# A mixture-of-experts stage with its chunk order changed: large and small experts in turn, down blocks queued behind

## The chip, the cores and the metric

The kernel runs on one core of a Trainium2 chip. The metric is the device time of one execution in microseconds (us). The engines are TensorE (PE, with its weight loads as PEld), VectorE (DVE), ScalarE (ACT), GpSimd (POOL) and SyncE (SP), whose queue (SPq) issues the loads from HBM.

## The reference

The program is a two-layer decoder trunk over 256 positions of width 1024. What matters here is the expert stage of the second layer and the gated embedding behind it:

```
logits = xt @ w_router;  gates = softmax(top-2 logits)
for each of 8 experts e, on the positions routed to it:
    g, u = split(xb @ w_gate_up[e])        # 1024 -> 2 x 3584
    y    = (silu(g) * u) @ w_down[e]       # 3584 -> 1024
h = h + sum of gate * y
h = h + (p @ w_proj) * sigmoid(rmsnorm(h) @ w_gate)
out = rmsnorm(h)
```

All of it is float32.

## The kernel before

**Products in parts.** TensorE works on pairs of fp32r values. `wsplit` makes such a pair from each raw weight tile, in steps of 128x1024: ACT copies the raw values to a rounded high part `wh` (line 145) and DVE subtracts it to give the low part `wl` (line 146). One such step is called a split below. It uses half a MB of weights. `wh` and `wl` have four buffers each (`SPL_BUFS`), and the raw tiles of 1 MB have eleven (`RAW_BUFS`); SP loads them in the order in which they are wanted. Activations are split by `split` (lines 197 and 198).

**Large and small experts.** Experts are ranked by how many positions they have. Places 0 to 3 have 128 slots (large), places 4 to 7 have 64 (small, `few(e)`). For a large expert `products` makes three products of a split and each output bank (high by high, low by high, high by low), so six matmuls of 512 columns for each split (line 174). For a small expert the high and low parts of its 64 slots lie side by side as 128 columns of the stationary operand, and two products do, so four matmuls for each split.

**Chunks.** The 3584 hidden columns are cut into chunks of 1024, 1024, 1024 and 512 (`CHUNKS`). `gate_up(e, c)` runs over 8 row blocks and gate and up, 16 splits (8 for the last chunk), into four PSUM banks of tag `a`, which are all there are. `activate` empties these: for a large expert ACT takes silu (line 1191) and DVE multiplies (line 1192); for a small one ACT copies all banks out (line 1188). `h_T` turns the hidden values for the down product, in pieces of 512 columns: a large one is transposed on PE (line 1220) and split; for a small one 16 small matmuls with `both` add the high and low half while they turn it, and then come silu on ACT (line 1211), a multiply on DVE (line 1212) and a split. All of these go through two PSUM banks of tag `t`. `down(e, c)` makes the products with the down weights, eight splits for 1024 rows, into two PSUM banks of tag `y` that an expert keeps over all its chunks. `combine` puts the expert's result back into `h` (line 1249).

**Order before.** The loop goes expert by expert and chunk by chunk. In each round PE gets the gate and up products of one chunk, and then the down products of the chunk before; `h_T` of the chunk before is called in `gate_up`, ahead of the second row block (`mid`). `activate` is called in the middle of the down products, after four of eight splits, and after two of four when the chunk before is the one of 512. The order of calls sets priorities; a scheduler decides at build time what each engine's queue holds, by its own estimates, so that matmuls of neighbouring steps are mixed in the queue. `gather` collects the positions of an expert pair (or of all four small experts) and `spread_slots` prepares the way back.

**Small tiles.** All small working tiles are of one size (2 KB for each partition) and share the tag `s2`, with twelve buffers. The products of the second embedding (`pj1`, four tiles) are made at the start of the expert stage and hold four of them until the end of the kernel. Some down weights are loaded into spare buffers of another tag (`SPARE`).

Of the kernel before, what the change touches and what calls it, by code (L numbers as in the profile page):

```python
# [8 lines left out]
F32 = mybir.dt.float32  # L9
# [7 lines left out]
P = 128  # L17
D = 1024
T = 256
NB = 2  # L20
# [4 lines left out]
NE = 8  # L25
# [58 lines left out]
def trunk_kernel(  # L84
# [88 lines left out]
    def mm(o, a, b, start, stop, shared=False):  # L173
        last["mm"] = pe.matmul(o, a, b, start=start, stop=stop, skip_group_check=shared)  # L174
# [768 lines left out]
    def layer1_moe(pT):  # L943
# [110 lines left out]
        def few(e):  # L1054
            return e >= FEW

# [105 lines left out]
        def products(e, triples, start, stop):  # L1162


            if not few(e):
                return mm3s(triples, start, stop)
            for part in range(2):
                for o, a, b in triples:
                    mm(o, a, b[part], start and part == 0, stop and part == 1)

        def gate_up(e, c, mid):
            ns = CHUNKS[c][1] // 512
            banks = [[pa(f"m{nm}{e}{c}{i}") for i in range(ns)] for nm in "gu"]
            for k, j, wt in gate_up_weights(e, c):
                if (k, j) == (MID, 0):
                    mid()
                products(e, [(banks[j][i], tokens[e][k], sub2(wt, slice(None), slice(i * 512, i * 512 + 512))) for i in range(ns)],
                         k == 0, k == KT - 1)

            def activate():  # L1180

                res = []
                with after("wcopy", "wsplit"):
                    for i in range(ns):
                        if few(e):
                            res.append([s2(f"ms{nm}{e}{c}{i}", [P, 512]) for nm in "gu"])
                            for j in range(2):
                                act.copy(res[i][j], banks[j][i])
                            continue
                        sg = s2(f"msg{e}{c}{i}", [P, 512])  # L1190
                        act.activation(sg, banks[0][i], AF.Silu)
                        dve.tensor_tensor(sg, banks[1][i], sg, MUL)
                        res.append(sg)
                return res

            return activate

        def h_T(e, c, sgs):

            res = []  # L1200

            for i, sg in enumerate(sgs):
                if few(e):

                    q = pt(f"mt{e}{c}{i}", (P, 2, 4, P // 2))
                    for j in range(2):
                        for g in range(2):
                            for k in range(2):
                                mm(q[:, j, 2 * g + k, :], sg[j][:, 256 * g + k : 256 * g + 256 : 2], both, True, True)
                    t = s2(f"mgu{e}{c}{i}", [P, 4, P // 2])  # L1210
                    act.activation(t, q[:, 0], AF.Silu)
                    dve.tensor_tensor(t, q[:, 1], t, MUL)
                    hT = s2(f"mh{e}{c}{i}", [P, 4, 2, P // 2], F32R)
                    split((hT[:, :, 0], hT[:, :, 1]), t)
                    res += [hT[:, k].rearrange("q i s -> q (i s)") for k in range(4)]
                    continue
                q = pt(f"mt{e}{c}{i}", (P, 4, P))
                for g in range(2):
                    for k in range(2):
                        pe.transpose(q[:, 2 * g + k, :], sg[:, 256 * g + k : 256 * g + 256 : 2], ident)  # L1220
                hT = (s2(f"mhh{e}{c}{i}", [P, 4, P], F32R), s2(f"mhl{e}{c}{i}", [P, 4, P], F32R))
                split(hT, q)
                res += [sub2(hT, slice(None), k) for k in range(4)]
            return res

        def down(e, c, hT, yb, between):

            c0, n = CHUNKS[c]
            res = None
            for g in range(n // 256):  # L1230
                nm = f"d{e}_{c}_{g}"
                view = expert(moe_w_down, e)[c0 + g * 256 : c0 + g * 256 + 256].rearrange("(q k) c -> q k c", k=2)
                wt = wload(view, (2, D), nm, spare(nm))
                for i in range(2):
                    products(e, [(yb[half], hT[2 * g + i], sub2(wt[i], slice(None), HALF[half])) for half in range(2)],
                             c == g == i == 0, c == len(CHUNKS) - 1 and g == n // 256 - 1 and i == 1)
                if g == n // 512 - 1 and between:
                    res = between()
            return res

        def combine(e, yb, half):
            s = slice(half * 512, half * 512 + 512)
# [8 lines left out]
        yb, hT = {}, {}  # L1251
        both = sm("both", (P, P // 2))
        dve.tensor_tensor(both, ident[:, : P // 2], ident[:, P // 2 :], ADD)

        def back(e, c, between=None):
            if c == 0:
                yb[e] = [py(f"y{e}{half}") for half in range(2)]
            if (e, c) == (NE - 1, len(CHUNKS) - 1):
                part = hT.pop((e, c))
# [11 lines left out]
            res = down(e, c, hT.pop((e, c)), yb[e], between)  # L1271
            if c == len(CHUNKS) - 1:
                for half in range(2):
                    combine(e, yb[e], half)
            return res

        def more_slots(e, pos):

# [58 lines left out]

            return over > P, more

        prev = None  # L1340
        for e in range(NE):
            for c in range(len(CHUNKS)):
                if e % 2 == 1 and c == 2 and e <= FEW - 1:
                    spread_slots = gather(e // 2 + 1)
                if (e, c) == (FEW, 1):
                    spread_slots()

                def mid():
                    if prev:
                        hT[prev] = h_T(*prev, sg)  # L1350
                    if (e, c) == (0, LATE):
                        for bn in todo:
                            product(*bn, pt)
                            copy(*bn)

                activate = gate_up(e, c, mid)
                if prev:
                    sg = back(*prev, activate)
                else:
                    sg = activate()  # L1360
                    with after("wsplit"):
                        gates()
                prev = e, c
        mid()
        last_norm = halves_norm_T("ple1")
        back(*prev)

        return pj1, (last_norm[0], last_norm[2]()), overflow

# [76 lines left out]


LAST_PIECES = ((0, 0, 512), (0, 512, 512), (1, 0, 512), (1, 512, 256), (1, 768, 256))
RAW_BUFS = 11
PAD = 8  # L1450
CONV_DVE = (31, 31, 5, 9)
MID = 1
FEW = 4
X_DVE = (3, 7)
PRODUCTS = (0, 2, 1, 0)
LATE = 1
CHUNKS = ((0, 1024), (1024, 1024), (2048, 1024), (3072, 512))
SPARE = ("gu0_0_0", "gu0_0_1", "d0_0_1", "d0_0_3", "d0_1_1", "d0_1_3", "d0_2_1", "d0_2_3", "d0_3_1", "d1_0_1", "d1_0_3")
S2_BUFS = 12
SPL_BUFS = 4  # L1460
SPL_COLS = 1024
XT_BUFS = 2
# [30 lines left out]
```

## Time and profile before

| | us |
|---|---|
| median of 3 runs (1496.48 to 1499.48) | 1496.91 |
| the profiled execution | 1497.28 |
| its span, first to last instruction | 1495.5 |
| PE, DVE, ACT busy in it | 1444.5, 1268.0, 1076.1 |

The span is what the trace covers; 1.8 us lie around it. Matmuls are pipelined and the ends of matmuls in the trace are modelled, so that the busy time of PE reaches the full length of a stretch before PE is at its peak: the distance from one start to the next is the safer measure.

### The profile page before, as it was taken

How to read it: one execution, taken by the hardware profiler on the slowest of the kernel's cores; microseconds unless marked ns; L12 is line 12 of the kernel's file. 1: busy time of each engine (PE TensorE's matmuls, PEld its weight loads, DVE VectorE, ACT ScalarE, POOL GpSimd, SP SyncE). 2: the span in 40 equal slices, each digit the busy share in tenths (PEclk: the TensorE clock that was granted, in tenths of full speed). 3: DMA queues.
4: the chain of work that ended last, by engine and by line, in shares of the span. 5: the costliest groups of instructions: out<-in, count | busy, mean ns of one | idle time of the engine just before them, and what ended most of it. 6: DMA issues, size and time to landing. Idle time of an engine off the chain costs nothing.

```text
span 1495.5 us, 22012 instructions
## 1 busy us (share of the span) xinstructions
PE 1444.5 (97%) x7726; PEld 1194.7 (80%) x7726; DVE 1268.0 (85%) x1716; ACT 1076.1 (72%) x1441; POOL 4.9 (0%) x14
## 2 busy tenths in 40 slices
PE   7999999999999999999999999999999999999996
PEld 6999899988888878888888888886766666666665
DVE  6778655556698699999999989989999999999997
ACT  6545544446547678887887877779988988988975
POOL 0000000000000000000000000000000000000000
PEclk9999999999999999999999999999999999999998
DMA  9614656555452469898898998999999999999961
GB/s 350 241 43 131 216 177 196 172 195 185 147 203 106 149 248 354 327 410 333 322 376 336 392 347 341 359 363 389 377 409 414 390 413 410 388 413 408 394 254 44
DMA packets 136610, 438.26 MB, mean 293 GB/s; under 512 B 9067, under 2 KB 34188, under 8 KB 122412
## 3 DMA queue, kind: packets, MB, share of 16 engines
q1 hardware_dynamic: 132960, 433.19, 77.3%
q10 hardware_dynamic: 3148, 2.31, 0.5%
q0 software_dynamic: 384, 1.29, 0.4%
q8 instruction: 62, 1.02, 0.3%
q14 instruction: 56, 0.46, 0.1%
HBM read 434.92 MB, written 1.84 MB: 292 GB/s over the span
## 4 chain that ended last, share of the span: by engine, by line
PE 71%; DVE 18%; issue 4%; ACT 4%; DMA 3%; ACTq 0%; DVEq 0%; POOL 0%; POOLq 0%
PE y L174 14%; PE mg L174 11%; PE mu L174 11%; DVE l L146 11%; PE fu L174 4%; PE fg L174 4%; PE fd L174 4%; PE wo L174 3%; PE pg L174 3%; PE mt L174 2%; DMA r_gu<-in_moe_w_gate_up_dram 2%; DVE l_d L146 2%; PE p L174 1%; PE mt L1220 1%; PE in_og L174 1%
## 5 line engine op out<-in xcount | busy, mean ns | idle before, releaser
L146 DVE TENSOR_TENSOR l<-r_gu,h 128x1024 fp32r<-128x1024 f32 x448 | 526.3, 1218 | 18.1 <-ACT h L145 6.3
L145 ACT CAST h<-r_gu 128x1024 fp32r<-128x1024 f32 x448 | 456.6, 1052 | 60.2 <-PE mu L174 22.4
L146 DVE TENSOR_TENSOR l_d<-r_d,h_d 128x1024 fp32r<-128x1024 f32 x220 | 258.6, 1219 | 16.7 <-ACT h_d L145 10.4
L145 ACT CAST h_d<-r_d 128x1024 fp32r<-128x1024 f32 x220 | 226.8, 1054 | 24.7 <-PE mu L174 10.3
L146 DVE TENSOR_TENSOR l_gu<-r_gu,h_gu 128x1024 fp32r<-128x1024 f32 x44 | 53.8, 1224 | 47.7 <-ACT h_gu L145 47.7
L145 ACT CAST h_gu<-r_gu 128x1024 fp32r<-128x1024 f32 x44 | 46.0, 1048 | 64.2 <-PE fu L174 49.0
L174 PE MATMUL y<-l_d,mh 128*128 128x512 f32 x216 | 75.3, 430 | 3.7 <-DVE l_d L146 3.7
L174 PE MATMUL y<-l_d,mhh 128*128 128x512 f32 x224 | 69.8, 393 | 0.1
L174 PE MATMUL y<-h_d,mh 128*128 128x512 f32 x216 | 69.2, 402 | 0.3
L174 PE MATMUL y<-h_d,mhh 128*128 128x512 f32 x224 | 69.4, 391 | 0.0
L174 PE MATMUL y<-h_d,mhl 128*128 128x512 f32 x224 | 69.1, 390 | 0.0
L174 PEld LDWEIGHTS y<-l_d,mh 128*128 128x128 f32 x216 | 34.4, 188 | 27.4 <-DVE l_d L146 25.1
L146 DVE TENSOR_TENSOR l_fd<-r_fd,h_fd 128x1024 fp32r<-128x1024 f32 x22 | 26.9, 1224 | 27.3 <-ACT h_fd L145 26.3
L174 PE MATMUL fg<-x_ffn0h,h_gu 128*128 128x256 f32 x176 | 49.9, 283 | 0.0
L174 PE MATMUL fu<-x_ffn0h,h_gu 128*128 128x256 f32 x176 | 49.9, 283 | 0.0
L174 PE MATMUL fg<-x_ffn0h,l_gu 128*128 128x256 f32 x176 | 49.9, 283 | 0.0
L174 PE MATMUL fu<-x_ffn0l,h_gu 128*128 128x256 f32 x176 | 49.8, 283 | 0.0
L174 PE MATMUL fu<-x_ffn0h,l_gu 128*128 128x256 f32 x176 | 49.8, 283 | 0.0
L174 PE MATMUL fg<-x_ffn0l,h_gu 128*128 128x256 f32 x176 | 49.8, 283 | 0.0
L174 PEld LDWEIGHTS y<-h_d,mhl 128*128 128x128 f32 x224 | 42.1, 188 | 8.9
L174 PEld LDWEIGHTS y<-l_d,mhh 128*128 128x128 f32 x224 | 41.5, 188 | 9.5 <-DVE l_d L146 1.4
L174 PEld LDWEIGHTS y<-h_d,mhh 128*128 128x128 f32 x224 | 41.8, 188 | 8.9 <-ACT h_d L145 0.4
(719 smaller groups left out, 3673.6 us busy)
## 6 DMA issues: line engine op xcount, KB each, us to landing
r_gu<-in_moe_w_gate_up_dram SPq DMA_DIRECT2D x192, 1024.0 KB, 7.7
r_d<-in_moe_w_down_dram SPq DMA_DIRECT2D x110, 1024.0 KB, 7.7
r_gu<-in_moe_w_gate_up_dram SPq DMA_DIRECT2D x64, 512.0 KB, 6.4
r_gu<-in_ffn_w_gate_up_dram SPq DMA_DIRECT2D x44, 512.0 KB, 4.4
r_fd<-in_ffn_w_down_dram SPq DMA_DIRECT2D x11, 1024.0 KB, 4.9
r_wo<-in_ev_w_out_dram SPq DMA_DIRECT2D x4, 1024.0 KB, 12.8
r_pg<-in_ple_w_gate_dram SPq DMA_DIRECT2D x4, 1024.0 KB, 7.0
r_wo<-in_od_w_out_dram SPq DMA_DIRECT2D x4, 1024.0 KB, 5.0
```

Of the source, the lines that this page charges most:

```text
L145: last["wcopy"] = act.copy(wh, raw[:, i : i + step])
L146: last["wsplit"] = dve.tensor_tensor(wl, raw[:, i : i + step], wh.bitcast(F32), SUB)
L174: last["mm"] = pe.matmul(o, a, b, start=start, stop=stop, skip_group_check=shared)
L1220: pe.transpose(q[:, 2 * g + k, :], sg[:, 256 * g + k : 256 * g + 256 : 2], ident)
```

## The change

The gate and up chunks are put in one list: a hand-written order for places 0 and 4 (`FIRST`), and then a chunk of a large expert and a chunk of a small one in turn, (1,0), (5,0), (1,1), (5,1) and so on. The down products are cut into blocks of 512 rows (four splits) and queued in the order of the experts 0, 4, 1, 5, 2, 6, 3, 7. Each step takes one gate and up chunk and behind it one or two blocks from this queue, which lags further and further behind: seven blocks of place 7 are left when the gate and up chunks are done. `h_T` is cut in two: `turn` (small matmuls, silu, multiply) is called for a small chunk in the step after its own, and what is left of `h_T` is called per block when the block's turn comes. `activate` is now called after two splits of the first block of a step. The gathers of the other experts move (`QUAD`, `SLOTS`, `PAIR`). The products `pj1` are stored to DRAM by four DMAs on ACT's queue and loaded again by SP ahead of the last block. There are 10 raw buffers for 11, 16 small ones for 12, and no spare buffers for down weights. The arithmetic is the same.

```
+        def turn(e, c):
+            sgs = hidden[e, c]
+            t = s2(f"mgu{e}{c}", [P, len(sgs), 4, P // 2])
             for i, sg in enumerate(sgs):
+                q = pt(f"mt{e}{c}{i}", (P, 2, 4, P // 2))
+                ... 16 x mm(q[:, j, 2 * g + k, :], sg[j][...], both, True, True)
+                act.activation(t[:, i], q[:, 0], AF.Silu)
+                dve.tensor_tensor(t[:, i], q[:, 1], t[:, i], MUL)
+            hidden[e, c] = t
...
-        def down(e, c, hT, yb, between):
+        def down(e, c, i, hT, yb, between):
-            for g in range(n // 256):
+            for g in range(2 * i, 2 * i + 2):
...
-                if g == n // 512 - 1 and between:
-                    res = between()
+                if g == 2 * i and between:
+                    between()
...
+        gates_up = [(e, c) for e, c in FIRST]
+        for e in range(1, FEW):
+            gates_up += [(i, c) for c in range(len(CHUNKS)) for i in (e, e + FEW)]
+        downs = [(i, c, n) for e in range(FEW) for i in (e, e + FEW) for c in range(len(CHUNKS)) for n in range(CHUNKS[c][1] // 512)]
+        stored = dr.tile([P, NB, 2, 512], F32, name="pj1d")
+        while gates_up or len(downs) > 1:
+            now = gates_up.pop(0) if gates_up else None
+            step = NE * len(CHUNKS) - len(gates_up) - 1 if now else None
+            n = next((i for i, d in enumerate(downs) if d[:2] not in hidden), len(downs))
+            n = min(2 if n > 2 or not now else 1, n, sum(d[0] == downs[0][0] for d in downs))
+            blocks, downs = downs[:n], downs[n:]
+            if step == QUAD:
+                spread_slots = gather(2)
+            if step == SLOTS:
+                spread_slots()
+            if step == PAIR:
+                gather(1)
+            def mid():
+                if fresh and few(fresh[0]):
+                    turn(*fresh)
+                for d in blocks:
+                    hT[d] = h_T(*d)
+                if now == (0, LATE):
...
+                    for b, i in BLOCKS:
+                        act.dma_start(stored[:, b, i], pj1[b][i])
...
         last_norm = halves_norm_T("ple1")
-        back(*prev)
+        for b, i in BLOCKS:
+            pj1[b][i] = s2(f"pj1{b}{i}", [P, 512])
+            sync.dma_start(pj1[b][i], stored[:, b, i])
+        hT[downs[0]] = h_T(*downs[0])
+        back(*downs[0])
...
-RAW_BUFS = 11
+RAW_BUFS = 10
+FIRST = ((0, 0), (0, 1), (4, 0), (0, 2), (4, 1), (0, 3), (4, 2), (4, 3))
+QUAD, SLOTS, PAIR = 1, 8, 15
-SPARE = ("gu0_0_0", "gu0_0_1", "d0_0_1", "d0_0_3", "d0_1_1", "d0_1_3", "d0_2_1", "d0_2_3", "d0_3_1", "d1_0_1", "d1_0_3")
-S2_BUFS = 12
+SPARE = ("gu0_0_0", "gu0_0_1")
+S2_BUFS = 16
```

## Rows read from the trace of the kernel before

**Rows 1.** Windows: stretch, length, PE, PEld, DVE, ACT, POOL busy, clock, DMA share, GB/s.

```profile
533.40:1000.00 466.60, 465.47 (x2127) 385.88 (x2126) 434.06 (x439) 371.27 (x402) 0.00 (x0) 1.00 0.94 354
1000.00:1454.70 454.70, 434.62 (x1917) 311.14 (x1916) 433.45 (x432) 394.27 (x477) 0.00 (x0) 1.00 0.99 391
801.00:921.00 120.00, 119.94 (x541) 99.33 (x541) 109.78 (x103) 93.91 (x100) 0.00 (x0) 1.00 0.96 364
1150.00:1260.00 110.00, 104.99 (x461) 74.03 (x459) 105.41 (x106) 95.94 (x116) 0.00 (x0) 1.00 1.02 405
```

**Rows 2.** Waits, 550 to 1000 us: total, times, longest.

```profile
ACT h L145 <- PE mu L174: 21.2, 64, 0.8
...
DVE mhl L198 <- ACT mhh L197: 5.8, 5, 2.5
```

**Rows 3.** Chain of waits, 500 to 600 us: a gather; a split's matmuls.

```profile
524.47 4.06 PE xg L174 x32
...
562.32 1.36 PE mu L174 x6
```

**Rows 4.** Timeline of PE: transposes (large); both kinds of matmul (small).

```profile
590.73 1.11 PE L1220 MATMUL mt<-cst,msg 128*128 128x128 f32 x8
591.59 0.70 PE L174 MATMUL mg<-h,xe0h 128*128 128x512 f32 x2
...
1103.34 0.39 PE L174 MATMUL mg<-l,xe2h 128*128 128x512 f32 x1
...
1104.25 0.39 PE L174 MATMUL mg<-l,xe2h 128*128 128x512 f32 x1
...
1445.24 0.81 PE L174 MATMUL mt<-both,msu 128*128 128x64 f32 x6
1445.86 0.48 PE L174 MATMUL y<-l_d,mh 128*128 128x512 f32 x1
```

**Rows 5.** Groups, 1010 to 1440 us: busy us, mean ns, idle us before.

```profile
L146 DVE TENSOR_TENSOR l<-r_gu,h 128x1024 fp32r<-128x1024 f32 x224 | 258.6, 1216 | 0.1
...
L146 DVE TENSOR_TENSOR l_d<-r_d,h_d 128x1024 fp32r<-128x1024 f32 x108 | 125.3, 1217 | 9.3 <-ACT h_d L145 9.3
...
L1212 DVE TENSOR_TENSOR mgu<-mt,mgu 128x256 f32<-128x256 f32 x27 | 11.4, 421 | 7.8 <-ACT mgu L1211 7.7
L198 DVE TENSOR_TENSOR mh<-mgu,mh 128x256 fp32r<-128x256 f32 x27 | 11.3, 417 | 0.1
```

**Rows 6.** Groups, 550 to 1000 us.

```profile
L198 DVE TENSOR_TENSOR mhl<-mt,mhh 128x512 fp32r<-128x512 f32 x27 | 17.9, 685 | 5.9 <-ACT mhh L197 5.8
L1192 DVE TENSOR_TENSOR msg<-mu,msg 128x512 f32<-128x512 f32 x27 | 17.4, 682 | 0.7 <-PE mu L174 0.7
```

**Rows 7.** Waits, 1010 to 1440 us.

```profile
ACT mgu L1211 <- PE mt L174: 32.7, 18, 3.4
...
ACT h L145 <- DMA r_gu<-in_moe_w_gate_up_dram: 0.9, 2, 0.6
```

**Rows 8.** DMA, 1150 to 1260 us; last figure: us to landing.

```profile
DMA packets 10779, 44.53 MB, mean 405 GB/s; under 512 B 739, under 2 KB 739, under 8 KB 8931
...
r_gu<-in_moe_w_gate_up_dram SPq DMA_DIRECT2D x24, 1024.0 KB, 8.3
```

**Rows 9.** Timeline, banks emptied after two splits: large expert; small expert (ACT, DVE).

```profile
790.47 1.07 ACT L1191 ACTIVATE msg<-mg 128x512 f32<-128x512 f32 x2
...
1140.64 0.58 ACT L1188 COPY msg<-mg 128x512 f32<-128x512 f32 x1 [0.84 <-PE mg L174]
...
1144.07 2.36 DVE L146 TENSOR_TENSOR l_d<-r_d,h_d 128x1024 fp32r<-128x1024 f32 x2 [0.86 <-ACT h_d L145]
```

**Rows 10.** Timeline of the end: last weight loads, last expert splits.

```profile
1433.82 2.97 SPq L167 DMA_DIRECT2D r_pg1h<-in_ple_w_gate_dram  x2
...
1450.06 4.62 DVE L146 TENSOR_TENSOR l_dl<-r_dl,h_dl 128x1024 fp32r<-128x1024 f32 x4
...
1469.64 1.22 DVE L146 TENSOR_TENSOR l_pg1h<-r_pg1h,h_pg1h 128x1024 fp32r<-128x1024 f32 x1 [0.21 <-ACT h_pg1h L145]
```

More of the change, by code (lines that the diff above doesn't have):

```diff
@@ L1196, in gate_up @@
             return activate
-        def h_T(e, c, sgs):
-            res = []
+        def turn(e, c):
+            sgs = hidden[e, c]
+            t = s2(f"mgu{e}{c}", [P, len(sgs), 4, P // 2])
             for i, sg in enumerate(sgs):
[L1203 to L1224, printed above, removed]
@@ L1226, in down, with h_T @@
-        def down(e, c, hT, yb, between):
+                q = pt(f"mt{e}{c}{i}", (P, 2, 4, P // 2))
+                for j in range(2):
+                    for g in range(2):
+                        for k in range(2):
+                            mm(q[:, j, 2 * g + k, :], sg[j][:, 256 * g + k : 256 * g + 256 : 2], both, True, True)
+                act.activation(t[:, i], q[:, 0], AF.Silu)
+                dve.tensor_tensor(t[:, i], q[:, 1], t[:, i], MUL)
+            hidden[e, c] = t
+        def h_T(e, c, i):
+            if few(e):
+                hT = s2(f"mh{e}{c}{i}", [P, 4, 2, P // 2], F32R)
+                split((hT[:, :, 0], hT[:, :, 1]), hidden[e, c][:, i])
+                return [hT[:, k].rearrange("q i s -> q (i s)") for k in range(4)]
+            q = pt(f"mt{e}{c}{i}", (P, 4, P))
+            for g in range(2):
+                for k in range(2):
+                    pe.transpose(q[:, 2 * g + k, :], hidden[e, c][i][:, 256 * g + k : 256 * g + 256 : 2], ident)
+            hT = (s2(f"mhh{e}{c}{i}", [P, 4, P], F32R), s2(f"mhl{e}{c}{i}", [P, 4, P], F32R))
+            split(hT, q)
+            return [sub2(hT, slice(None), k) for k in range(4)]
@@ L1228, in down @@
+        def down(e, c, i, hT, yb, between):
             c0, n = CHUNKS[c]
-            res = None
-            for g in range(n // 256):
+            for g in range(2 * i, 2 * i + 2):
                 nm = f"d{e}_{c}_{g}"
@@ L1233, in down @@
                 wt = wload(view, (2, D), nm, spare(nm))
-                for i in range(2):
-                    products(e, [(yb[half], hT[2 * g + i], sub2(wt[i], slice(None), HALF[half])) for half in range(2)],
-                             c == g == i == 0, c == len(CHUNKS) - 1 and g == n // 256 - 1 and i == 1)
-                if g == n // 512 - 1 and between:
-                    res = between()
-            return res
+                for k in range(2):
+                    products(e, [(yb[half], hT[2 * (g % 2) + k], sub2(wt[k], slice(None), HALF[half])) for half in range(2)],
+                             c == g == k == 0, c == len(CHUNKS) - 1 and g == n // 256 - 1 and k == 1)
+                if g == 2 * i and between:
+                    between()
         def combine(e, yb, half):
@@ L1249, in combine, with back @@
                 dve.scalar_tensor_tensor(h[:, b, s], q, Gr[:, b, e : e + 1], h[:, b, s], MUL, ADD)
-        yb, hT = {}, {}
+        yb, hT, hidden = {}, {}, {}
         both = sm("both", (P, P // 2))
         dve.tensor_tensor(both, ident[:, : P // 2], ident[:, P // 2 :], ADD)
-        def back(e, c, between=None):
-            if c == 0:
+        def back(e, c, i, between=None):
+            if c == i == 0:
                 yb[e] = [py(f"y{e}{half}") for half in range(2)]
+            part = hT.pop((e, c, i))
             if (e, c) == (NE - 1, len(CHUNKS) - 1):
-                part = hT.pop((e, c))
                 rows = expert(moe_w_down, e)[CHUNKS[c][0] :].rearrange("(g q k) c -> g q k c", k=2, q=P)
@@ L1270, in back @@
                 return
-            res = down(e, c, hT.pop((e, c)), yb[e], between)
+            down(e, c, i, part, yb[e], between)
             if c == len(CHUNKS) - 1:
@@ L1274, in back @@
                     combine(e, yb[e], half)
-            return res
         def more_slots(e, pos):
@@ L1338, in overflow @@
             return over > P, more
[L1340 to L1363, printed above, removed]
@@ L1364, in layer1_moe, with between @@
-        mid()
-        last_norm = halves_norm_T("ple1")
-        back(*prev)
+        gates_up = [(e, c) for e, c in FIRST]
[3 more added lines that the diff above has]
+        stored = dr.tile([P, NB, 2, 512], F32, name="pj1d")
+        fresh = None
+        while gates_up or len(downs) > 1:
[16 more added lines that the diff above has]
+                if now == (0, LATE):
+                    for bn in todo:
+                        product(*bn, pt)
+                        copy(*bn)
+                    for b, i in BLOCKS:
+                        act.dma_start(stored[:, b, i], pj1[b][i])
+            if now:
+                activate = gate_up(*now, mid)
+                def between(now=now, activate=activate):
+                    hidden[now] = activate()
+            else:
+                mid()
+                between = None
+            for i, d in enumerate(blocks):
+                back(*d, between if i == 0 else None)
+            if not blocks:
+                between()
+            if step == 0:
+                with after("wsplit"):
+                    gates()
+            fresh = now
```

## The prediction

> **What bounds the kernel now.** I read the windows first, cut where the large experts give way to the small ones. From the first unbroken split at 533.4 us to the last expert split, which begins its run of four at 1450.1 and is done at 1454.7 [rows 10], the expert stage lasts 921.3 us, and it has two halves, the first two rows; the other two are one large and one small expert [rows 1]. In the large half PE is busy for its whole length and DVE for 434.1 of 466.6 us: DVE idles 32.5. In the small half DVE works 433.5 of 454.7 us and idles 21.3. DVE has 867.5 us of work in all, and 53.8 us of idle time is the most that any order of this work can win if DVE's work stays what it is.
>
> Then the waits say who holds whom. In the large half ACT waits for PE to give back split buffers, in the largest group 64 times for 21.2 us [rows 2]: PE is the slow one. In the small half DVE waits for ACT, and ACT for the small matmuls `mt`, 18 times for 32.7 us, while weights are late for 0.9 us only [rows 7].
>
> Last come the prices, which say whether the two halves fit into each other. A split costs PE 1.36 us at a large expert [rows 3] and 1104.25 - 1103.34 = 0.91 at a small one [rows 4]. DVE's price is (258.6 + 125.3) / (224 + 108) = 1.16 us for either [rows 5], between the two. PE needs 84 x 1.36 = 114.2 for a large expert, 3.0 for 28 transposes (0.86 / 8 each [rows 4]) and 1.8 for eight `combine` matmuls of 0.23, so 119.0, and the window of one shows 120 [rows 1]. A small one needs 84 x 0.91 = 76.4, 112 small matmuls at 0.62 / 6 = 0.10 for 11.6 [rows 4], and 1.8: 89.8 in a window of 110. The mean of the two is 104.4; DVE's mean is (109.8 + 105.4) / 2 = 107.6 [rows 1]. Mixed finely enough, DVE is the bound and PE fits under it. By its busy time PE would not fit half so well: 465.5 + 434.6 = 900.1 us, 21 under the stage. The starts decide here, since the ends of matmuls are modelled.
>
> The Trainium skill (Perfetto Trace Analysis, Identifying the Most-Contended Engine) says the same: matmul busy time is a poor measure and the busy share of weight loads a better one. The weight loads here are busy 99.3 of 120 us at a large and 74.0 of 110 us at a small expert [rows 1]. By matmul busy time the gain would end at 21 us, by starts at 53.8.
>
> **The change, part by part.** *Order of the chunks.* Take the eight steps of places 2 and 6, 168 splits. A large chunk of 16 splits costs PE 21.8, DVE 18.5 and two multiplies of 0.64 [rows 6], 19.8. A small chunk is 14.6 against 18.5. A large down block is PE 5.4 + 0.4 against DVE 4.6 + 0.66 [rows 6]; a small one 3.6 against 4.6 + 0.42 [rows 5]. A `turn` of two pieces is 3.3 against 0.84. PE less DVE in the eight steps is then +0.5, -6.7, +1.7, -7, +5.7, -2.7, +4.1, -3. DVE may be ahead by four split buffers, 4.6 us. Only the fifth and the seventh step go past that, by 1.1 and 1.4, so DVE waits 2.5 us per pair of experts and 10 for four. If DVE may lead by two splits only, it is 5.2 per pair, 21. But DVE's small waits let PE catch up, so it may be 0. I take 5. The 32.5 us of idle in the large half become 5.
>
> *Emptying the banks after two splits.* Before, this was so only behind a 512 chunk. There the small expert shows ACT waiting 0.84 us for the last gate products, then copying four banks, and DVE idle 0.86 us [rows 9]. Of the twelve small chunks of 1024, four were in that place; eight more cost 8 x 0.86 = 6.9 us. Behind ACT's copies the splits of the next weights queue, and DVE waits for those. At a large expert silu came without a wait [rows 9]: 0. The ends are 0 and 12 x 0.86 = 10.3.
>
> *`turn` and `h_T`.* They issue the same instructions in other places, the waits of ACT for `mt` included; I leave the small half's 21.3 us as they are, with 0 as the other end. In the steps (2,2) and (3,2) four pieces go through two `t` banks; the price lies between 0 and 2 x 3.4, the longest such wait [rows 7]; I take 0, since the scheduler puts matmuls between them.
>
> *The end.* Seven down blocks of place 7 come last, with gate and up long done. The chain from the last gate matmul through `mt` to the last down products is no longer on the path; the wait that stands for it, DVE's for ACT's silu, was 7.7 us in all [rows 5] and 0.3 for each of 27 pieces; with the matmuls ahead of it I take 1 us.
>
> *`pj1` by way of DRAM.* Four stores and four loads of 256 KB are 2.1 MB, 5.2 us of DMA at 405 GB/s [rows 8]. DMA is ahead: the last gate weights of the second embedding are issued by 1436.8 and used at 1469.6 [rows 10], so 33 us less 8.3 to land [rows 8]. SP's four loads stand ahead of the last weights and wait for small buffers, of which `pj1` holds none of 16 now, where it held four of 12; 0, and 2.6 us if that cover were gone. ACT's four issues fall in the large half's start, where ACT waits for PE.
>
> *Buffers and gathers.* One raw buffer less is 2.3 us of DVE's work; a load lands after 8.3 us, 3.6 buffers, and ten are left: 0. Each gather costs PE 4.1 us [rows 3], before and after alike.
>
> **The sum.** 32.5 - 5 - 6.9 + 1 = 21.6 us. From the profiled execution's 1497.3 that is 1475.7, so 1476. That execution lies 0.4 above the median of the runs, which changes nothing.
>
> **The rivals.** *DVE's waits go too.* With PE's work spread, the small half's 21.3 us could shrink to some 5 as well, and the time to 1497.3 - 48 = 1449. For it: down products no longer wait for hidden values just made. Against it: the same `mt` stand in ACT's queue.
>
> *The feed becomes the bound.* Rows 1 give 354 x 466.6 + 391 x 454.7 = 343 MB, and 2.1 for `pj1`. In the large half the DMA engines are 0.94 busy at 354 GB/s; if that meant a limit of 376, the stage would need 918 us and the time would be 1494. Against it: 405 GB/s at a small expert and almost no wait for weights [rows 7, 8]; at 405 the stage needs 852.
>
> The Trainium skill (DMA: Bandwidth & Descriptors, Specifications) gives a core some 358 GB/s of HBM; by that the stage would take an estimated 964 us, and the kernel 1540. The trace's 405 is above it, so I give this no more than 1 in 100, inside the next chance.
>
> *Slower: ACT reaches the banks too early at large chunks.* After a large chunk PE is up to four splits behind, and `activate` now stands two splits behind the last gate split. If ACT's queue holds it there, ACT waits 2 x 1.36 = 2.7 us at each of 16 large chunks, and DVE with it: 43.5 us. Then the gain of 21.6 turns into 1497.3 - 21.6 + 43.5 = 1519 at worst; it is slower from 1.35 us per chunk. For it: the small expert's 0.84 us wait [rows 9]. Against it: at the large expert the scheduler had moved another split ahead and silu came without a wait.
>
> *Nothing comes of it.* PE and DVE stay coupled by four buffers, and what the large half gains is given back in the small steps: 1497.
>
> **How the numbers follow.** A measurement of this kernel tells some 0.2% (3 us) from no change. The forecast, a gain of 9 to 33 us with a range of its own of 1464 to 1488, has 0.56; DVE's waits gone as well, around 1449, 0.11; the feed, around 1491 to 1494, 0.10; no change 0.08; slower, 1501 to 1519, 0.15. The range that leaves out no more than 2 in 10 runs from 1455 to 1494: below it lies part of the second case, above it no change and the slower one. Faster is 0.56 + 0.11 + 0.10 = 0.77.
>
> **What would show it.** If I am right, DVE is busy some 96% of the whole expert stage, the stage lasts about 900 us, ACT's short waits for split buffers shrink to a few us, and the weights flow at some 380 GB/s throughout instead of 354 and then 391. The waits of ACT for `mt` stay, and DVE shows idle times of just under 1 us after small chunks. I would be wrong if ACT's wait for gate products before silu grows (slower), if ACT waits for loads (the feed), or if DVE's idle time stays near 54 us.

## The result and the profile after

The changed kernel takes 1517.89 us (median of 4 runs, 1517.57 to 1518.7) against 1496.7 for the kernel before beside it: a ratio of 1.0139, with a 95% interval of 1.0121 to 1.0156. It is slower by 21 us, where 21.6 us less were forecast. The profiled execution took 1518.7 us with a span of 1516.9.

The windows of the kernel after: the expert stage, and the two windows that answer to the last of [rows 1]. The columns are as there.

```profile
534.70:1478.00 943.30, 910.37 (x4045) 701.01 (x4043) 863.74 (x869) 763.43 (x878) 1.06 (x2) 0.99 0.96 368
801.00:921.00 120.00, 116.19 (x517) 89.46 (x516) 109.53 (x104) 95.73 (x107) 0.00 (x0) 1.00 0.98 373
1150.00:1260.00 110.00, 106.95 (x488) 83.38 (x488) 99.30 (x98) 85.79 (x100) 0.00 (x0) 1.00 0.97 371
```

DVE's work is what it was, 863.7 us for 867.5, but the stage lasts 943.3 us for 921.3: DVE idles 79.6 us where it idled 53.8. These 22 us make up the difference of the spans, 21.4: the stage also begins 1.3 us later, and what follows it is shorter. Both windows look alike now, as mixing should make them, and in the second DVE works 99.3 us where it worked 105.4.

The waits of the kernel after, for the stretches of [rows 2] and [rows 7] (total, times, longest); first 550 to 1000 us:

```profile
ACT mgu L1210 <- PE mt L174: 22.9, 13, 3.5
...
DVE mgu L1211 <- ACT mgu L1210: 11.1, 10, 1.9
ACT h L145 <- PE mu L174: 10.1, 27, 1.2
```

and 1010 to 1440 us:

```profile
ACT mgu L1210 <- PE mt L174: 27.6, 13, 3.5
...
DVE mgu L1211 <- ACT mgu L1210: 13.4, 11, 1.6
ACT mhh L197 <- PE mt L1223: 11.9, 10, 3.5
DVE l_d L146 <- ACT h_d L145: 8.7, 15, 0.9
```

ACT's wait for split buffers in the first stretch fell from 21.2 to 10.1 us in its largest group; the forecast had it at a few us. In its place stands ACT's wait for the small matmuls before the turn's silu, and DVE's for that silu. No wait of ACT for a load is in either list. The timeline of ACT and then DVE at one turn of the kernel after, and a little before it, shows how it comes to that (the last bracket is idle time before, and what ended it):

```profile
1094.11 1.05 ACT L145 CAST h<-r_gu 128x1024 fp32r<-128x1024 f32 x1 [0.81 <-DVE l L146]
1097.69 0.38 ACT L1210 ACTIVATE mgu<-mt 128x256 f32<-128x256 f32 x1 [2.53 <-PE mt L174]
1099.57 0.39 ACT L1210 ACTIVATE mgu<-mt 128x256 f32<-128x256 f32 x1 [1.50 <-PE mt L174]
1099.85 1.04 ACT L145 CAST h<-r_gu 128x1024 fp32r<-128x1024 f32 x1
...
1084.46 2.36 DVE L146 TENSOR_TENSOR l_d<-r_d,h_d 128x1024 fp32r<-128x1024 f32 x2 [0.86 <-ACT h_d L145]
...
1098.10 0.42 DVE L1211 TENSOR_TENSOR mgu<-mt,mgu 128x256 f32<-128x256 f32 x1 [0.15 <-ACT mgu L1210]
1099.99 0.42 DVE L1211 TENSOR_TENSOR mgu<-mt,mgu 128x256 f32<-128x256 f32 x1 [1.46 <-ACT mgu L1210]
```

ACT makes no weight copy from 1095.2 to 1099.85 us: it stands at the first silu, and then, with nothing between, at the second. DVE runs out of copies. Behind emptied banks the idle time of the forecast is there too (0.86 us at 1084.46).

The end is as forecast or better. The last expert split of the kernel after:

```profile
1477.04 1.22 DVE L146 TENSOR_TENSOR l_dl<-r_dl,h_dl 128x1024 fp32r<-128x1024 f32 x1 [0.26 <-ACT h_dl L145]
```

From its end at 1478.3 to the end of the span (1516.9) are 38.6 us; before they were 1495.5 - 1454.7 = 40.8. The forecast had 1 us less.

### The profile page after: what moved, and what is told of

It reads as the page before. It is cut to its first block, busy times and chain, and to the rows that moved or that the text cites. A ratio compares the mean times of both kernels' runs of the same rounds, so it can differ in the third digit from the quotient of the medians.

```text
span 1516.9 us, 22009 instructions
## 1 busy us (share of the span) xinstructions
PE 1455.3 (96%) x7726; PEld 1199.2 (79%) x7726; DVE 1264.1 (83%) x1716; ACT 1073.7 (71%) x1441; POOL 4.9 (0%) x14
## 4 chain that ended last, share of the span: by engine, by line
PE 69%; DVE 19%; ACT 5%; issue 4%; DMA 2%; ACTq 0%; DVEq 0%; POOL 0%; POOLq 0%
PE mg L174 12%; PE y L174 12%; PE mu L174 12%; DVE l L146 10%; PE fu L174 4%; PE fg L174 4%; DVE l_d L146 4%; PE fd L174 4%; PE mt L174 3%; PE wo L174 3%; PE pg L174 3%; PE p L174 1%; ACT h_d L145 1%; ACT h L145 1%; PE pj L174 1%
## 5 line engine op out<-in xcount | busy, mean ns | idle before, releaser
L146 DVE TENSOR_TENSOR l<-r_gu,h 128x1024 fp32r<-128x1024 f32 x448 | 520.1, 1219 | 12.7 <-ACT h L145 8.3
L145 ACT CAST h<-r_gu 128x1024 fp32r<-128x1024 f32 x448 | 455.7, 1053 | 45.4 <-PE mu L174 17.1
L146 DVE TENSOR_TENSOR l_d<-r_d,h_d 128x1024 fp32r<-128x1024 f32 x220 | 257.9, 1220 | 21.2 <-ACT h_d L145 18.5
L145 ACT CAST h_d<-r_d 128x1024 fp32r<-128x1024 f32 x220 | 221.8, 1054 | 15.6 <-PE mu L174 5.3
L146 DVE TENSOR_TENSOR l_gu<-r_gu,h_gu 128x1024 fp32r<-128x1024 f32 x44 | 53.8, 1224 | 47.7 <-ACT h_gu L145 47.7
L1210 ACT ACTIVATE mgu<-mt 128x256 f32<-128x256 f32 x28 | 10.8, 385 | 56.8 <-PE mt L174 56.8
L174 PEld LDWEIGHTS y<-h_d,mh 128*128 128x128 f32 x216 | 40.6, 192 | 12.6 <-ACT h_d L145 2.4
L146 DVE TENSOR_TENSOR l_fd<-r_fd,h_fd 128x1024 fp32r<-128x1024 f32 x22 | 26.9, 1225 | 27.3 <-ACT h_fd L145 26.3
```

Of the source, the lines that this page charges most:

```text
L145: last["wcopy"] = act.copy(wh, raw[:, i : i + step])
L146: last["wsplit"] = dve.tensor_tensor(wl, raw[:, i : i + step], wh.bitcast(F32), SUB)
L1210: act.activation(t[:, i], q[:, 0], AF.Silu)
```

## The experiments

The first theory, **turn**: ACT works through its queue in order and stands at the turn's silu until PE has worked off the products ahead of the small matmuls; mixing large products in makes PE later there. The rivals: **banks** (they are emptied two splits too early) and **coupling** (four split buffers are too few for PE's swing). The kernel before took 1496.9 to 1498.4 us beside the runs. Runs with one time each are told apart only where they differ by more than 3 us.

**Banks emptied later** (e1).

```
-                if g == 2 * i and between:
+                if g == 2 * i + late and between:        # late = len(blocks) - 1
```

> The changed kernel with one part undone: activate is called after four of eight splits where a step has two down blocks, as in the kernel before. Theory 'turn' (ACT's queue stands at the silu of turn, whose small matmuls PE has queued among its products): this changes little, 1512 to 1519 us, and DVE's idle time ahead of mgu stays near 27 us. Theory 'banks' (activate two splits behind the last gate product makes ACT wait for PE): ACT's waits for mg, 24.6 us, fall to under 10, and the time to 1500 to 1508. Theory 'coupling' (four split buffers cannot carry the mix, whatever ACT waits for): no change, 1516 to 1520.

1515.79 us. That is 2.1 less than the change, too little to tell from no change. ACT's wait for mt rose from 56.8 to 63.7 us, while its wait for gate products at the banks fell from 24.6 to 10.1: the wait moved on to the turn.

**The turn's silu held back** (e2): `turn` issues its small matmuls in one place, and silu and multiply follow behind the copies of the fourth row block; `h_T` comes ahead of it.

```
+            def finish():
+                for i, q in enumerate(qs):
+                    with after("wcopy"):
+                        act.activation(t[:, i], q[:, 0], AF.Silu)
+                    dve.tensor_tensor(t[:, i], q[:, 1], t[:, i], MUL)
...
+                if (k, j) == (PIN, 0):                   # PIN = 3
+                    pinned()
```

> The changed kernel with the silu and multiply of turn held back: the small matmuls stay ahead of the second row block, and ACT's silu is put behind the copies of the fourth row block; h_T of the blocks comes ahead of turn. Theory 'turn': ACT's waits for mt fall from 57 us to under 15, DVE's idle time ahead of mgu from 27 us to under 8, and the time to 1490 to 1500. Theory 'banks': no more than 5 us gained, 1512 to 1518. Theory 'coupling': DVE waits elsewhere as long, 1514 to 1520.

1504.49 us, 13.4 less than the change; with *turn* alone I had expected 1490 to 1500.

**No wait for the small matmuls** (e3): silu and multiply read the copied gate and up values, and the matmuls' result is not used, so that the values are not turned.

```
-                act.activation(t[:, i], q[:, 0], AF.Silu)
+                act.activation(t[:, i], sg[0][:, :256].rearrange(...), AF.Silu)
```

> The changed kernel in which turn's silu and multiply read the copied gate and up values and not the result of the small matmuls; the small matmuls are issued all the same, and nothing reads them. Part of the computation is left out with that: the small experts' hidden values are not turned. ACT has no wait for mt any more. Theory 'turn': 1488 to 1500 us. Theory 'banks': 1510 to 1518. Theory 'coupling': 1512 to 1520.

1508.52 us, where *turn* alone would have given 1488 to 1500: not as good as e2, though the turn waits for nothing. ACT now stood at the next of its operations that need PE. The waits of e3, 533 to 1450 us:

```profile
ACT mhh L197 <- PE mt L1223: 39.0, 19, 4.9
DVE mhl L198 <- ACT mhh L197: 21.0, 13, 2.9
```

It was 16.1 and 8.2 us for these in the kernel after. So the wait that was taken away at one place came back, in large part, at another.

**The kernel before with its banks emptied after two splits everywhere** (e4).

```
-                if g == n // 512 - 1 and between:
+                if g == 0 and between:
```

> The kernel before with one part of the change: activate is called after the first two splits of the down chunk everywhere. Theory 'banks': some 24 chunks pay 0.5 to 1 us each, 1508 to 1520 us. Theories 'turn' and 'coupling': 1495 to 1503.

1497.9 us, no change, where *banks* needed 1508 or more. The waits of e4, 533 to 1450 us:

```profile
DVE l_d L146 <- ACT h_d L145: 19.0, 32, 2.3
ACT mgu L1211 <- PE mt L174: 18.9, 19, 2.0
...
DVE mgu L1212 <- ACT mgu L1211: 2.3, 4, 0.6
```

In the kernel before these were 10.4, 36.0 and 8.7 us. DVE's 8.6 us more behind the banks are there, but ACT then waits 17.1 us less for the small matmuls, and the turn gives DVE 6.4 us back.

**e1 and e2 together** (e5), the two edits above in one kernel.

> The two changes of the earlier runs together: the banks are emptied after four of eight splits where a step has two blocks, and the turn's silu is held back behind the copies of the fourth row block. If the two costs are separate, the gains of 13.4 us (silu held back) and 2.1 us (banks later) add up to about 1502. If ACT's wait only moves to the next of its operations that needs PE (the large blocks' h_T, the banks), the second change gives nothing here: 1504 to 1508, and ACT's wait for mt before mhh stays at 20 us or grows.

1506.35 us: the gains do not add. *Banks* falls as a cause.

**The old order of chunks and blocks, all else as in the change** (e6).

```
-        gates_up = [(e, c) for e, c in FIRST]
-        ...
+        gates_up = [(e, c) for e in range(NE) for c in range(len(CHUNKS))]
+        downs = [(i, c, n) for i in range(NE) for c ...]
-QUAD, SLOTS, PAIR = 1, 8, 15
+QUAD, SLOTS, PAIR = 14, 17, 6
```

> The chunks and the down blocks in the old order, expert by expert, the gathers where they were; all the rest of the change stays (blocks of 512 rows in a lagging queue, turn one step later, banks emptied after two splits, pj1 in DRAM, the new buffers). If it is the mixing of large and small work that makes ACT's small operations wait for PE (PE behind by up to four splits at each turn), the time falls back to 1497 +- 4 and ACT's wait for mt before the turn's silu to some 33 us or less. If the rest of the change is the cause (the place of turn, the blocks, the buffers), it stays at 1512 to 1520.

1518.84 us. Had mixing been the cause, it would have been 1497. Mixing is not what makes the change slow: without it the time is the same, and in the window of the small expert (1150 to 1260) DVE works 100.4 us, where it worked 105.4 in the kernel before. The waits of e6, 533 to 1450 us:

```profile
ACT mgu L1210 <- PE mt L174: 36.9, 27, 2.0
...
DVE mgu L1211 <- ACT mgu L1210: 20.2, 15, 1.6
```

In the kernel before these were 36.0 and 8.7 us. ACT waits hardly longer at the turn than it did, and yet DVE waits 11.5 us more for the silus.

**Six split buffers, eight raw ones** (e7).

```
-RAW_BUFS = 10
+RAW_BUFS = 8
-SPL_BUFS = 4
+SPL_BUFS = 6
```

> Six buffers for the high and low parts in place of four, and eight raw buffers for ten; the order is that of the change. If the loss is the swing of PE's work against a lead of four splits, six buffers take up the swing: DVE idles 30 us or more less, about 1485. If ACT stands at a small operation until PE has worked off what is ahead of it, a longer lead means a longer backlog at the same place: no gain, 1513 to 1525, and the longest wait of the turn's silu grows from 3.5 to 4 us and more. If eight raw buffers are too few, ACT shows waits for loads.

1516.26 us. ACT's wait for mt grew to 61.4 us, and its wait for gate products at the banks from 24.6 to 72.7: at the same operations ACT waits longer, as would follow if a longer lead means a longer backlog of products in front of them.

**Everything that reads a t bank held back** (e8): as e2, and the split of a large block's `h_T` behind the copies of the fourth row block, the turn's silu behind those of the sixth; in the last steps turn follows the blocks.

```
+                if j == 0 and k in PINS:                 # PINS = (3, 5)
+                    pins[PINS.index(k)]()
```

> Each operation of ACT that reads a t bank gets a place two row blocks (four copies) behind its matmuls: the large blocks' h_T is transposed at the second row block and copied behind the copies of the fourth, the turn's small matmuls come there and their silu behind the copies of the sixth; in the last steps turn comes behind the blocks. If ACT's standing at t banks is the loss, its waits for mt fall below 10 us, DVE idles 45 us or less in the stage, and the time is 1475 to 1490. If the wait moves on (to the emptying of the banks, 26 us with the silu alone held back, or to PE, which must keep its two t banks free), the time stays at 1500 to 1506.

1496.75 us: 21 less than the change, and level with the kernel before. I had expected either 1475 to 1490 or 1500 to 1506. Holding these readings back makes good the whole loss; but the kernel before gains by the same treatment too (e12 below), so not all of it is the change's own.

**The old order with later banks** (e9) and **with all t readings held back** (e10); the edits are those of e6 with e1's, and of e6 with e8's.

> The old order of chunks and blocks again, the rest as in the change, but the banks are emptied after four of eight splits where a step has two blocks, as it was before. If emptying the banks two splits earlier is what costs 20 us in the old order too (ACT waited 16.6 us there for gate products), the time falls to 1497 to 1503. If it is the place of turn and of the blocks, it stays at 1512 to 1519 and ACT's wait for mt does not fall below 35 us.

> The old order of chunks and blocks, with every operation of ACT that reads a t bank held back behind later copies, as in the run of the mixed order that took 1496.75. If mixing large and small work is worth something by itself, this one is slower than that by 10 us or more: 1507 to 1515. If mixing is worth nothing, it is 1497 +- 4; if mixing costs, because PE runs up to four splits behind and catches up in turn, it is 1480 to 1492, since then the small half's waits are gone and only the large half's idle time stays.

1519.24 us and 1490.9 us (ratio to the kernel before 0.9955, 0.9938 to 0.9971). Held back, the old order is 5.9 us ahead of the mixed one.

**The mixed order held back farther** (e11: e8 with e1's edit, and chunks of 512 with PINS 4 and 7), and **the kernel before held back** (e12: order, buffers and the rest as before).

```
+PINS = (4, 7), (3, 5)                                    # e11
+                    one.append((first, i, q))            # e12: silu and multiply, at the first pin
...
+                one.append((split, hT, q))               # e12: split of a large piece
...
+                two.append((second, i, t))               # e12: split of a small piece, at the second
```

> The change with every reading of a t bank held back, in the chunks of 512 too by three copies and not by one or two, and the banks emptied after four of eight splits where a step has two blocks. The run without the last two had DVE idle 2.3 us at each turn after a chunk of 512 (three times) and 0.86 us nine times behind emptied banks. If these places are separate costs, some 10 to 14 us go: 1483 to 1488. If PE's swing of up to four splits is what stays and only finds other places, 1494 to 1500.

> The kernel before, with its order and its buffers, where only the readings of the t banks are held back: the silu and the multiply of a small piece, and the split of a large one, behind the copies of the fourth row block (the fifth row block of a chunk of 512), the split of a small one two row blocks later. If ACT's standing at t banks costs the kernel before too, DVE's idle time of 8.7 us (turn) and 8.1 us (large blocks) goes and the time is 1480 to 1490. If these waits were covered by work that PE and DVE could not have done faster anyway, it is 1494 to 1500.

e11 took 1496.15 us (0.9989, 0.998 to 0.9999). e12 took 1487.96 us (0.9934, 0.9918 to 0.9951), better than both kernels, and 8.8 us ahead of e8, the mixed order so treated. Its small half, in the windows of e12, and its waits (533 to 1450 us):

```profile
1000.00:1446.40 446.40, 423.91 (x1916) 314.43 (x1915) 432.61 (x431) 390.21 (x477) 0.00 (x0) 1.00 1.00 397
```

```profile
ACT mgu L1216 <- PE mt L174: 12.4, 8, 2.0
...
DVE mgu L1217 <- ACT mgu L1216: 0.5, 1, 0.5
```

The half of [rows 1] that took 454.7 us takes 446.4 (its windows end with the last expert split in each), and DVE idles 13.8 us in it for 21.3.

**What in the rest of the change makes the wait dearer.** ACT's queue tells: in the kernel before, two or three weight copies and a split stand between the two silus of a turn, since each piece is split before the next; in the change `turn` makes both silus first. e13 puts that one cut into the kernel before, e14 and e15 take it out of the change (the old order of e9, the mixed order of e1), e16 gives the kernel before the change's buffer numbers.

```
+            t2 = s2(f"mgu{e}{c}", [P, len(sgs), 4, P // 2]) if few(e) else None      # e13
...
-                    act.activation(t, q[:, 0], AF.Silu)
-                    dve.tensor_tensor(t, q[:, 1], t, MUL)
+                    act.activation(t2[:, i], q[:, 0], AF.Silu)
+                    dve.tensor_tensor(t2[:, i], q[:, 1], t2[:, i], MUL)
+            for i, sg in enumerate(sgs):
+                if few(e):
                     hT = s2(f"mh{e}{c}{i}", [P, 4, 2, P // 2], F32R)
-                    split((hT[:, :, 0], hT[:, :, 1]), t)
+                    split((hT[:, :, 0], hT[:, :, 1]), t2[:, i])
```

```
+                split((hT[:, :, 0], hT[:, :, 1]), t)     # e14, e15: in turn's loop, behind the multiply
...
-RAW_BUFS = 11
+RAW_BUFS = 10                                            # e16
...
-S2_BUFS = 12
+S2_BUFS = 16
```

> The kernel before with one edit: for a small chunk both pieces first go through small matmuls, silu and multiply, and only then are both split, as the change's turn does; in ACT's queue the two silus then stand next to each other, where two or three weight copies and a split stood between them. If this cut is the cause of the loss, the time is 1510 to 1518, and DVE's wait for the turn's silu goes from 8.7 us to 20 us and more. If the loss comes from elsewhere (the lagging queue of blocks, the buffers), 1496 to 1500.

> The change in the old order of chunks and blocks, the banks emptied after four of eight splits, and turn going piece by piece again: small matmuls, silu, multiply and split of the first piece ahead of the second. Without the last edit this kernel took 1519.2. If the cut is the cause, the time falls to 1496 to 1502, and DVE's wait for the turn's silu from 27.6 us to about 9. If the cause is elsewhere, 1512 to 1520.

> The mixed order of the change with turn going piece by piece and the banks emptied after four of eight splits; without the first edit it took 1515.8. If the cut costs the mixed order as much as the old one, 1496 to 1502. If PE, which is further behind where a large chunk's products lie ahead, makes even the first silu wait, only a part comes back: 1503 to 1512.

> The kernel before with the buffers of the change: ten raw, sixteen small, no spare buffers for down weights; order and turn as before. If these are worth nothing, as the forecast had it, 1496 to 1499 (a measurement tells 3 us). If ten raw buffers starve ACT, it shows waits for loads and 1502 or more.

1521.67, 1499.22, 1503.71 and 1497.9 us; the kernel before took 1496.87 beside them. The cut alone makes the kernel before 24.8 us slower (1510 to 1518 were expected); without it the old order is 20.0 us faster (1519.24 to 1499.22) and the mixed one 12.1 (1515.79 to 1503.71). The buffers do nothing. One turn in the timeline of the kernel before, ACT and then DVE:

```profile
1206.62 0.38 ACT L1211 ACTIVATE mgu<-mt 128x256 f32<-128x256 f32 x1 [2.00 <-PE mt L174]
1206.90 1.98 ACT L145 CAST h_d<-r_d 128x1024 fp32r<-128x1024 f32 x2
1208.78 1.05 ACT L145 CAST h<-r_gu 128x1024 fp32r<-128x1024 f32 x1
1209.73 0.40 ACT L197 CAST mh<-mgu 128x256 fp32r<-128x256 f32 x1
1210.04 0.38 ACT L1211 ACTIVATE mgu<-mt 128x256 f32<-128x256 f32 x1
...
1207.03 0.42 DVE L1212 TENSOR_TENSOR mgu<-mt,mgu 128x256 f32<-128x256 f32 x1 [0.58 <-ACT mgu L1211]
1207.97 2.36 DVE L146 TENSOR_TENSOR l_d<-r_d,h_d 128x1024 fp32r<-128x1024 f32 x2 [0.51 <-ACT h_d L145]
```

and the same turn in e13:

```profile
1216.52 0.38 ACT L1210 ACTIVATE mgu<-mt 128x256 f32<-128x256 f32 x1 [1.99 <-PE mt L174]
1218.85 0.39 ACT L1210 ACTIVATE mgu<-mt 128x256 f32<-128x256 f32 x1 [1.95 <-PE mt L174]
1219.13 1.99 ACT L145 CAST h_d<-r_d 128x1024 fp32r<-128x1024 f32 x2
...
1216.93 0.42 DVE L1211 TENSOR_TENSOR mgu<-mt,mgu 128x256 f32<-128x256 f32 x1 [0.57 <-ACT mgu L1210]
1220.21 2.36 DVE L146 TENSOR_TENSOR l_d<-r_d,h_d 128x1024 fp32r<-128x1024 f32 x2 [2.85 <-ACT h_d L145]
```

The first silu waits alike. In the kernel before, three copies follow it, DVE has work, and the second silu finds its matmuls done. In e13 it waits 1.95 us, and DVE idles 0.57 + 2.85 = 3.42 us where it idled 1.09. Twelve chunks of 1024 at these 2.33 us more would be an estimated 28 us; 24.8 were measured. Most of the idle time is not where I had looked for it: from 533 to 1480 us, DVE's wait for the silus grew from 8.7 to 13.6 us (20 and more were expected), and its wait for the down copies behind them from 10.4 to 28.5. The Trainium skill (Perfetto Trace Analysis, Tensor Engine Instruction) calls the queues of ACT and DVE strictly first in, first out, while PE can pull weight loads ahead; e13's trace agrees for ACT, since the copies behind the second silu had no wait of their own and yet began only after it, at 1219.13.

**Six split buffers with everything held back**, three row blocks behind (e17 mixed, e18 old order): the edits of e7 and e8, for e18 those of e6 too. Buffers and places change together here.

```
-PINS = (3, 5)
+PINS = (4, 7)
```

> The mixed order with every reading of a t bank held back, three row blocks behind its matmuls, and six split buffers with eight raw ones. With four buffers and two row blocks it took 1496.75, 5.9 us more than the old order so treated. If PE's swing of up to four splits is what eats the gain of mixing, six buffers give the mixed order 8 us or more, 1480 to 1489, and it is no longer behind the old order. If the mixed order loses elsewhere (turns behind chunks of 512, banks), it stays at 1493 to 1500.

> The old order in the same treatment, six split buffers and eight raw ones; with four it took 1490.9. In the old order each half has one and the same ratio of PE's work to DVE's, so more buffers should give little: 1487 to 1493 in either case. It is the measure for the mixed order's run beside it.

1491.47 and 1483.84 us. Both gain, by 5.3 and 7.1 us, so the mixed order stays behind, by 7.6; the old order had been expected at 1487 to 1493, as having little to gain. A pair of experts in the mixed order takes nearly the same time with four buffers as with six; the windows from turn to turn of the kernel after, of e8 and of e17, in this order:

```profile
1163.39:1398.00 234.61, 226.35 (x998) 172.98 (x997) 214.54 (x209) 188.85 (x215) 0.00 (x0) 1.00 0.98 377
```

```profile
1156.31:1384.65 228.34, 222.34 (x998) 174.01 (x997) 214.85 (x209) 189.94 (x215) 0.00 (x0) 1.00 1.00 387
```

```profile
1154.90:1382.62 227.72, 221.94 (x998) 174.17 (x997) 212.83 (x208) 184.31 (x215) 0.00 (x0) 1.00 1.00 388
```

DVE idles 13.5 us per pair in e8. *Coupling* as I had it falls. DVE's longest idle times in e8's pair:

```profile
1187.84 0.69 DVE L198 TENSOR_TENSOR yl<-y,yh 128x512 fp32r<-128x512 f32 x1 [1.44 <-ACT yh L197]
1243.17 2.36 DVE L146 TENSOR_TENSOR l_d<-r_d,h_d 128x1024 fp32r<-128x1024 f32 x2 [0.86 <-ACT h_d L145]
1273.76 1.29 DVE L1194 TENSOR_TENSOR msg<-mu,msg 128x512 f32<-128x512 f32 x2 [0.70 <-PE mu L174]
...
1384.65 0.42 DVE L1220 TENSOR_TENSOR mgu<-mt,mgu 128x256 f32<-128x256 f32 x1 [2.31 <-ACT mgu L1219]
```

They stand at the end of a large expert, behind emptied banks, at the multiplies of large chunks and at the turn behind the chunk of 512. In e17's pair the longest are 4.28 us at the same turn, and 2.49 and 1.92 us at multiplies of large chunks: again fixed places where ACT or DVE waits for PE, each longer by 1.2 to 2.0 us. e18 is the fastest of all, on one time.

## Why the prediction was wrong

**What bounds it: right in part.** DVE's work stayed, and DVE less idle in the stage would have been the gain. But "Mixed finely enough, DVE is the bound and PE fits under it" did not come: in e8's pair of 228.3 us DVE idles 13.5 us, and PE, at the forecast's own prices (119.0 and 89.8), an estimated 19.5.

Two steps failed. Undone one after the other in the mixed order, the parts of the change cost 2.1 us (banks, e1), 12.1 (the cut, e15), 4.5 (mixing, e14) and 2.3 (all the rest, e14 against the kernel before): 21.0 in all, of which the first and the last are too small to tell from nothing. The parts do not add in every order: in the old order the cut costs 20.0.

**The first step that failed: `turn` and `h_T`.** I wrote that they "issue the same instructions in other places" and left the small half's idle time as it was. The instructions are the same, but in ACT's queue the copies that stood between the two silus are gone, and that was their cover. This alone is 24.8 us in the kernel before (e13); with the rest of the change it is 12.1 in the mixed order (e15) and 20.0 in the old one (e14). The diff showed it: the split left the loop over the pieces. I costed the operations and their waits, 32.7 us, and not what ACT had done between them. At the turn shown, a wait of ACT of 2.00 us cost DVE 1.09 where copies followed it, and 3.94 in two waits in a row cost it 3.42.

**The second: the order of the chunks, the term of 32.5 down to 5.** It is the larger miss: 27.5 us of gain were forecast. The pair's DVE work is as worked out (214.85 us in e8, 215.2 forecast), and ACT's wait for split buffers shrank. But in like treatment the mixed order took 4.5 (e15 with e14), 5.9 (e8 with e10) and 7.6 us (e17 with e18) more than the old one; only with the cut in place was it no slower (1517.89 with 1518.84 in e6, 1515.79 in e1 with 1519.24 in e9). The forecast gave a pair 2.5 us of DVE's idle time for the order and 1.7 for the banks; e8, where DVE's wait for the turn's silu is down to 7.8 us from 26.9, has 13.5. I had bounded the swing by the buffers' lead; the lost time sits instead at the operations of ACT and DVE that need PE: of e8's 13.5 us, 2.8 at the turn, 4.4 at the banks (the multiplies included) and 1.4 at the expert's end, the rest in smaller pieces. What makes PE late at just these places was not tried by itself. Whether another place for each of them would let mixing gain is open: e11 tried one, and it did not.

**Emptying the banks: size right, worth wrong.** 6.9 us were forecast; DVE's wait for down copies grew by 8.6 us in e4 and by 7.6 in the change. But undoing it gives 2.1 us (e1) or nothing (e9), within what one time can tell, as the turn's wait takes it up. Here, idle times that follow one another on one engine did not add.

**The end, buffers, `pj1`: right at about 0.** The end came out 2.2 us shorter, where 1 was forecast; e16 shows the buffers at 1497.9. A cost of `pj1` by way of DRAM was not tried by itself; e14, which has it, took 2.3 us more than the kernel before, which one time cannot tell from nothing.

**The rivals.** The slower one named 1519 at worst, near the result, but that is chance. Its sign came, as ACT's wait for gate products before the large experts' silu grew from 1.0 to 11.9 us; but over 13 times that is 0.9 each, under its own point of 1.35, and with the banks emptied later (e1) the time stayed. The feed never bound: no wait of ACT for a load is left in the stage. The Trainium skill (DMA: Bandwidth & Descriptors, Specifications) has 358 GB/s for a core; e18 moved 407 over its small half (1000 to 1440 us). The Trainium skill (HBM Reference, Specifications) has about 425 for a core that streams alone; e18 lies between the two.

## What to carry to other kernels

In an engine that works in order, price an operation that waits for another engine by the independent work that stands between it and the last such wait; here two in a row cost what two with work between them did not. Issue such operations some copies behind their producers, all of them, since a wait that was taken away at one place came back at the next (e3): here that made the kernel before 0.66% faster by itself. When a diff moves one step out of a loop, write out the consumer's queue before and after. And that the sums of two engines' work fit under one another does not say that mixing will bring the time down to them.

## What the runs showed of the hardware

The granted clock fell once inside the expert stage of the kernel after, where it was 0.99 or 1.00 in every window of 10 us outside 1435 to 1455. The windows of the kernel after around the last turn, and PE's timeline there:

```profile
1423.00:1436.00 13.00, 12.55 (x53) 9.44 (x52) 10.94 (x11) 9.78 (x13) 0.00 (x0) 1.00 1.00 401
1436.00:1444.00 8.00, 5.24 (x21) 4.16 (x20) 6.23 (x8) 1.84 (x2) 0.00 (x0) 0.77 0.72 246
1444.00:1451.00 7.00, 5.74 (x15) 4.40 (x15) 4.89 (x9) 5.19 (x10) 0.00 (x0) 0.53 0.79 281
1451.00:1464.00 13.00, 13.00 (x55) 9.43 (x53) 12.79 (x12) 12.71 (x14) 0.00 (x0) 1.00 0.90 305
```

```profile
1437.53 1.06 PE L174 MATMUL cb<-yh,ohT 128*128 128x512 f32 x2 [1.50 <-DVE h L1249]
...
1440.49 1.97 PE L174 MATMUL mt<-both,msg 128*128 128x64 f32 x8 [1.06 <-DVE h L1249]
1442.26 1.91 PE L174 MATMUL mt<-both,msu 128*128 128x64 f32 x8
1445.43 1.22 PE L174 MATMUL y<-h_d,mh 128*128 128x512 f32 x2 [1.26 <-DVE mh L198]
...
1450.68 0.63 PE L174 MATMUL y<-h_d,mh 128*128 128x512 f32 x2
1451.15 0.62 PE L174 MATMUL y<-l_d,mh 128*128 128x512 f32 x2
```

PE had waited 1.50 us at 1437.53, and then 1.06 and 1.26 us as shown; the clock went to about half (1.2 of 2.4 GHz) and was back by 1451, products having followed one another from 1445.43 on. Two products of 512 columns took 1.22 us, and 0.62 afterwards. The holes in PE's work were paid for a second time: the twelve products that began from 1445.43 to 1450.68 took 5.25 us, where at the later distance of 0.47 for two they would have taken 2.8, so my estimate is 2.4 us of PE's time. What part of it reached the time of the kernel is not shown.
